# A gate's matmuls moved into the attention's tail, the first rows on earlier bytes, gate scaling on ScalarE, and the first cross norms inside the last product of the output projection

## The chip, the cores and the metric

The kernel runs on one core of a Trainium2 chip. The metric is device microseconds of one execution: before the change 2441.82 us, the median of three runs (2439.93 to 2442.28). The engines are TensorE (PE in the profile; its weight loads are PEld), VectorE (DVE), ScalarE (ACT), GpSimd (POOL) and the two queues that start transfers here, SyncE's (SPq) and ScalarE's (ACTq).

## The reference, cut to what matters

One layer of a hybrid encoder, 1024 tokens by 1024 channels, all in float32:

```python
h = rmsnorm(x, norm_mix);  proj = h @ w_in            # q k v | z | x B C | dt | gate_a | gate_b
attn = windowed_gqa_sink(q, k, v, sink)               # 16 heads, |t-s| <= 128, ALiBi, sink logit
ssd  = ssd_branch(z, xbc, dt, ...)                    # two scans, 2048 channels
merged = sigmoid(gate_a) * (attn @ w_attn_branch) + sigmoid(gate_b) * (ssd @ w_ssd_branch)
x = x + merged @ w_out                                # "wo"
h = rmsnorm(x, norm_cross)
x = x + cross_attention(h, rmsnorm(mem, norm_mem), w_xq, w_xkv, w_xo)
x = x + square(relu(rmsnorm(x, norm_ffn) @ w_up)) @ w_down
out = rmsnorm(x, norm_final)
```

The change lies between the end of `attn` and the first products of `cross_attention`.

## The kernel before, in words

Products keep float32 accuracy by splitting each operand into a high half (rounded to the matmul's format) and a low half (the rest), and by issuing three matmuls: high by high, high by low, low by high. A weight of 128 by 1024 is made ready by `wload` and `split_in` (L60 to L75): a transfer into a `raw` tile (2 buffers) on SPq, a copy to the high half on ACT (L66), a subtraction for the low half on POOL (L67); the two halves take two of the 6 `wop` buffers. Activations are split by an ACT copy and a DVE subtraction.

**Attention** (`attn_phase`, L584): four groups of heads. Each computes q and k, then for eight blocks of 128 queries the scores (L667, L668), the softmax (DVE L669, ACT L675, POOL L680), transposes (L690), a split (ACT L693, DVE L694) and the values (L699, L700), and writes the block to DRAM (L707). After each group comes one gate block (`gate_block`, `ATT_GATES`): 48 matmuls of h by a slice of `w_in`, a tanh and a store. Here the order on all engines is made by a planner that works through a priority heap in program order with estimated durations, so a gate's matmuls fill places where it expects PE to be idle. All tiles of this phase lie in one pool, `p2`, on the left side of the on-chip memory.

**Merge** (`merge_phase`, L719). On PE the order is now the written one; the other engines and the SP queue keep the planner's order. Four steps follow each other:

1. The gates 14 and 15 (`END_GATES`, 96 matmuls, L735 to L742), while the rows of the first product are loaded: `Pair.load(j)`, j = 0 to 7, one row of y and one of `w_ssd_branch` each, 16 rows of 512 KB. The rows with j < 4 lie in `k1` (10 buffers in the pool `m3`, which reuses the bytes of `p2`), the others in `k2` (right side) and `wop`.
2. Two `Pair`s for `ssd @ w_ssd_branch`. A `Pair` is a product of two 1024-deep halves done in seven half-size products (Strassen-Winograd form, `ORDER` = 1, 2, 6, 5, 7, 3, 4), of 48 matmuls each (L1399). The operands of the next product are sums of quarters (`op`, L1316, DVE) and splits (`split`, ACT L1350 and DVE L1351), dealt out as `units` between the four groups of matmuls. The first product takes only rows with j < 4; `early(j)` makes four sums from the rows j and 4 + j.
3. `attn @ w_attn_branch`: two halves h of eight steps m, of 24 matmuls each. Each step needs one weight `wa` (`wa_load`, two steps ahead), and multiplies its result by a gate: `gate(m, h)` (L771) fetches a tile `g` (4 buffers) on SPq, and POOL turns the stored tanh into the sigmoid (L774). In the half h = 0 each step also splits a piece of `attn` for the other half (`at_split`), fetches and applies two gates 8 + m to the accumulator, and issues `p.load(m)` for `w_out` and the load of a row of x. In the half h = 1 each step does one of the eight units of the first split of `wo` (`split1`), and sums of `early`.
4. `merged @ w_out` as a third `Pair`, added into x.

**Cross attention** (`cross_phase`, L845): the planner orders PE again. Four norms and transposes of the rows 0 to 3 of x (`norm_tile`, L131, with its helpers up to L152: a square with sum on ACT, L127; a scale on DVE, L118; a power on POOL, L120; a product on DVE, L139; eight transposes on PE, L148; the split on ACT, L151, and DVE, L152), the splits of the keys and values kx and vx (two `wload`s with halves in `p3`), then `xq_unit(0, i)` (24 matmuls each on all four transposed rows) in turn with the norms of the rows 4 to 7. The norms' results `xn` of the rows 0 to 3 share two buffers (`ld`).

Of the kernel before, what the change touches and what calls it, by code (L numbers as in the profile page):

```python
# [16 lines left out]
P = 128  # L17
S = 1024
# [11 lines left out]
ATT_GATES = ((10,), (11,), (12,), (13,))  # L30
END_GATES = (14, 15)
# [552 lines left out]
def attn_phase(kx, ins, dr):  # L584
    nc, tc = kx.nc, kx.tc
    V, A, G, PE = nc.vector, nc.scalar, nc.gpsimd, nc.tensor
    with tc.tile_pool(name="p2", bufs=1) as ap:
# [31 lines left out]
        for kv in range(4):  # L619
            if kv % 2 == 0:  # L620
                w = wload(kx, ins["wk"][kv // 2])
                ps = kx.pg.tile([P, S], F32, tag="g", name="kps")
                for h in range(2):
                    gemm_fm(kx, ps[:, h * 512:(h + 1) * 512], w, kx.hT[h])
                for s in range(2):
                    kh = ap.tile([P, S], F32R, tag="kh", bufs=2, name="kh")
                    kl = ap.tile([P, S], F32R, tag="kl", bufs=2, name="kl")
# [91 lines left out]
def merge_phase(kx, ins, dr, x1_open):  # L719
# [4 lines left out]
    with tc.tile_pool(name="m3", bufs=1, reuse_waits="tile") as fp, ExitStack() as right, \  # L724
            tc.manual_schedule(engines={mybir.EngineType.PE}):
        k2p = right.enter_context(tc.tile_pool(name="m3r", bufs=1, side="right", reuse_waits="tile"))
        acc = [fp.tile([P, S], F32, tag="acc", bufs=8, name="acc") for _ in range(8)]
        pools = {"k1": fp, "k2": k2p}
        pairs = [Pair(kx, fp, pools, ins["wsb"][8 * b:8 * b + 8], dr.y[8 * b:8 * b + 8]) for b in range(2)]
# [5 lines left out]
        gw = [wload(kx, ins["wg"][m]) for m in END_GATES]  # L735
        for j in range(8):
            p.load(j)
        gps = [[bank() for _ in range(2)] for _ in END_GATES]
        pin_next_matmul(kx)
        for h in range(2):  # L740
            for w, ps in zip(gw, gps):
                gemm_fm(kx, ps[h], w, kx.hT[h])  # L742
        for m, ps in zip(END_GATES, gps):
            gt = kx.tabp.tile([P, 2, 512], F32, tag="tab", bufs=1, name="gt")
            for h in range(2):
                A.activation(gt[:, h], ps[h], AF.Tanh, scale=0.5)
                nc.scalar.dma_start(dr.gt[m][h], gt[:, h])
# [22 lines left out]

        def gate(m, h):  # L771
            g = fp.tile([P, 512], F32, tag="g", bufs=4, name="g")
            nc.sync.dma_start(g, dr.gt[m][h])
            G.tensor_scalar(g, g, 1.0, 0.5, ALU.add, ALU.mult)  # L774
            return g
# [25 lines left out]
        right.close()  # L801
        atk[1] = act_tiles(kx)
        kx.x1 = []
        x1p = x1_open()
        p = Pair(kx, fp, pools, None, [ins["wo"][k] for k in range(8)], acc)
        split1, early = None, None
        for h in range(2):
            for m in range(8):
                if h == 0:
                    at_split(1, m)  # L810
                    for hh in range(2):
                        g = gate(8 + m, hh)
                        V.tensor_tensor(half(m, hh), half(m, hh), g, ALU.mult)
# [21 lines left out]
                if 8 * h + m + 2 < 16:  # L835
                    wa_load((m + 2) % 8)

# [4 lines left out]
        p.products(bank, lambda i: p.units(i, None), add)  # L842


def cross_phase(kx, ins, dr):  # L845
    nc, tc = kx.nc, kx.tc
    V, A, G, PE = nc.vector, nc.scalar, nc.gpsimd, nc.tensor
    with tc.tile_pool(name="p3", bufs=1, reuse_waits="tile") as mp:
# [6 lines left out]
        def norm(h, j, grow, dst):  # L855
            xn = t4f("xn") if grow is not g_cross else mp.tile([P, D], F32, tag="ld", bufs=2, name="xn")
            norm_tile(kx, mp, kx.x1[4 * h + j], xn, grow, dst[h], j * P)

        g_cross = load_row(kx, kx.tabp, ins["gcross"], "tab")
        h2T = [act_tiles(kx)]  # L860
        for j in range(4):
            norm(0, j, g_cross, h2T)
# [6 lines left out]
        kxh, kxl = split_kv(dr.kx, "kx")  # L869
        vxh, vxl = split_kv(dr.vx, "vx")  # L870
# [414 lines left out]
class Pair:  # L1285
# [5 lines left out]
    def __init__(self, kx, fp, pools, us, ws, u=None):  # L1291
        self.kx, self.fp, self.pools, self.us, self.ws = kx, fp, pools, us, ws
        self.u, self.w, self.xy = u or [None] * 8, [None] * 8, [None] * 4

    def row(self, tag, src):
        if tag == "wop":
            t = self.kx.wp.tile([P, D], F32, tag="wop", bufs=6, name="row")
        else:
            t = self.pools[tag].tile([P, D], F32, tag=tag, bufs={"k1": 10, "k2": 6}[tag], name="row")
# [3 lines left out]
    def load(self, j):  # L1303
        if self.us is not None:
            self.u[j] = self.row("k1" if j < 4 else "k2", self.us[j])
        self.w[j] = self.row("k1" if j < 4 or self.us is None else "wop", self.ws[j])
# [11 lines left out]
    def early(self, j):  # L1318
# [5 lines left out]
        else:  # L1324
            self.xy[j] = self.fp.tile([P, D], F32, tag="k1", bufs=10, name="xy")
# [79 lines left out]
def down_phase(kx, ins, dr, first, out):  # L1405
    nc, tc = kx.nc, kx.tc
    V, A, G, PE = nc.vector, nc.scalar, nc.gpsimd, nc.tensor
    with tc.tile_pool(name="p6", bufs=1, reuse_waits="tile") as fp, \
# [21 lines left out]
        pairs = [Pair(kx, fp, {"k1": fp, "k2": fp}, dr.u[m:m + 8], [ins["wdn"][k] for k in range(m, m + 8)])  # L1430
                 for m in (16, 24, 4)]
# [24 lines left out]
        for b, p in enumerate(pairs):  # L1456
            nxt = pairs[b + 1] if b < 2 else None
            if nxt is None:
                fraw, fw, fu = [None] * 8, [], []

                def fload(j):
                    fraw[j] = p.row("wop", ins["wdn"][12 + j])
                    fraw[4 + j] = p.row("k2", dr.u[12 + j])
# [38 lines left out]
def hybrid_encoder(ctx, tc, ins, out, dbg=None):  # L1502
# [33 lines left out]
    with tc.tile_pool(name="tabp", bufs=1) as kx.tabp:  # L1536
# [9 lines left out]
        merge_phase(kx, ins, dr, x1_open)  # L1546
        ok, grow = cross_phase(kx, ins, dr)
# [77 lines left out]
```

## Time and profile before

| | us |
|---|---|
| median of three runs | 2441.82 |
| the profiled execution | 2442.35 |
| its span, first to last instruction | 2440.6 |
| PE busy | 2339.8 (96%) |
| DVE, ACT, POOL busy | 1606.9, 1134.5, 928.9 |
| granted TensorE clock, mean | 0.988 |

A line of the timeline gives the start of an instruction (or of a run of like ones, xN), its duration, engine, source line, operation, output<-inputs, sizes, and in brackets the idle time of the engine just before it with what ended it. A line of the windows gives, for one stretch, the busy time and the number of instructions of each engine, the granted TensorE clock, the busy share of the DMA engines and their rate. Times are microseconds from the span's start.

### The profile page before, as it was taken

The page shows a single profiled execution, that of the slowest core. Times are in us where ns is not written, and L with a number is a line of the kernel's source. Part 1 is how long each engine was busy: PE and PEld are TensorE (multiplying, and loading weights), DVE is VectorE, ACT ScalarE, POOL GpSimd, SP SyncE. Part 2 cuts the span into 40 slices and gives each one's busy share as a digit, 9 for nine tenths or more (in the row PEclk, how much of TensorE's full clock was granted, in tenths as well). Part 3 has the DMA queues.
Part 4 walks back from the last instruction along what each step waited for, and adds up shares of the span by engine and source line. Part 5 has one row for each costly group of instructions (what it writes and reads, how often), then busy time and mean ns, then how long its engine had stood idle before and what let it go on. Part 6 is the DMA issues. An engine that isn't in the chain of part 4 may idle for free.

```text
span 2440.6 us, 32397 instructions
## 1 busy us (share of the span) xinstructions
PE 2339.8 (96%) x11868; PEld 1941.6 (80%) x11868; DVE 1606.9 (66%) x2520; ACT 1134.5 (46%) x2406; POOL 928.9 (38%) x873
## 2 busy tenths in 40 slices
PE   7899999999999998999989999999998999999998
PEld 6687887878788787877767887878986887788887
DVE  5747576575756655356657888874676446689984
ACT  5436354454635444477765442244553333233442
POOL 4235445363543525245441015324485444200010
PEclk9999999999999999999999999999999999999999
DMA  6214132231413223111116256212243335731301
GB/s 220 81 61 128 55 112 87 73 115 57 127 57 110 82 77 97 40 52 49 41 42 224 104 168 228 70 44 70 86 152 133 104 121 160 255 155 70 130 26 69
DMA packets 150319, 252.07 MB, mean 103 GB/s; under 512 B 11280, under 2 KB 86160, under 8 KB 150160
## 3 DMA queue, kind: packets, MB, share of 16 engines
q1 hardware_dynamic: 79264, 211.19, 25.5%
q10 hardware_dynamic: 70896, 38.81, 5.6%
q8 instruction: 94, 1.54, 0.3%
q14 instruction: 65, 0.53, 0.1%
HBM read 202.51 MB, written 47.45 MB: 102 GB/s over the span
## 4 chain that ended last, share of the span: by engine, by line
PE 60%; DVE 14%; POOL 9%; ACT 8%; issue 6%; DMA 3%; ACTq 0%; POOLq 0%; SPq 0%; DVEq 0%
PE dps L1399 9%; PE mps L1399 8%; PE pb L1191 6%; PE pc L1191 3%; PE zp L85 2%; PE zp L81 2%; PE zp L86 2%; PE st L462 2%; POOL wlo L67 2%; DVE cx L350 2%; POOL prev L477 2%; POOL cb_t L476 1%; ACT whi L66 1%; PE dps L85 1%; PE dps L81 1%
## 5 line engine op out<-in xcount | busy, mean ns | idle before, releaser
L67 POOL TENSOR_TENSOR wlo<-raw,whi 128x1024 fp32r<-128x1024 f32 x110 | 271.9, 2473 | 471.8 <-ACT whi L66 442.5
L1350 ACT ACTIVATE kt<-row 128x512 fp32r<-128x512 f32 x264 | 144.2, 620 | 187.3 <-PE dps L1399 82.9
L1399 PE MATMUL mps<-kt 128*128 128x512 f32 x1008 | 229.0, 389 | 0.0
L1399 PE MATMUL dps<-kt 128*128 128x512 f32 x1008 | 228.6, 389 | 0.0
L81 PE MATMUL cps<-kt,whi 128*128 128x512 f32 x512 | 217.1, 424 | 8.6 <-DVE cx L350 8.6
L1399 PEld LDWEIGHTS mps<-kt 128*128 128x128 f32 x1008 | 189.2, 188 | 39.5 <-DVE kt L1351 0.4
L1399 PEld LDWEIGHTS dps<-kt 128*128 128x128 f32 x1008 | 189.2, 188 | 39.3
L66 ACT ACTIVATE whi<-raw 128x1024 fp32r<-128x1024 f32 x112 | 118.0, 1055 | 199.2 <-DMA raw<-in_wa_dram 48.8
L86 PE MATMUL cps<-kt,wlo 128*128 128x512 f32 x512 | 200.8, 392 | 0.0
L85 PE MATMUL cps<-kt,whi 128*128 128x512 f32 x512 | 200.4, 391 | 0.0
L1351 DVE TENSOR_TENSOR kt<-row,kt 128x512 fp32r<-128x512 f32 x264 | 176.3, 715 | 7.1 <-ACT kt L1350 7.0
L81 PEld LDWEIGHTS cps<-kt,whi 128*128 128x128 f32 x512 | 97.1, 190 | 34.9 <-issue 16.3
L120 POOL TENSOR_TENSOR rr<-rv,mhalf 128x1 f32<-128x1 f32 (+1 forms) x50 | 38.5, 771 | 220.9 <-DVE rv L118 218.1
L1137 POOL TENSOR_TENSOR wop<-w,wop 128x512 fp32r<-128x512 f32 x64 | 86.1, 1346 | 85.9 <-ACT wop L1136 74.4
L85 PEld LDWEIGHTS cps<-kt,whi 128*128 128x128 f32 x512 | 97.1, 190 | 26.1 <-issue 7.3
L86 PEld LDWEIGHTS cps<-kt,wlo 128*128 128x128 f32 x512 | 96.8, 189 | 21.0
L496 ACT ACTIVATE ef<-rows,ebias 128x128 f32<-128x128 f32 x256 | 83.2, 390 | 53.3 <-PE cb L511 49.8
L1191 PE MATMUL pb<-kt,wop 128*128 128x512 f32 x384 | 96.3, 399 | 11.0 <-ACT c L1245 9.4
L669 DVE CUSTOM_DVE_ANT_0 t<-sps,bias 128x384 f32<-128x384 f32 (+1 forms) x128 | 64.3, 521 | 55.1 <-PE sps L668 53.7
L497 ACT ACTIVATE eb<-rows,ebias 128x128 f32<-128x128 f32 x256 | 84.3, 392 | 34.9 <-POOL rows L488 34.9
L680 POOL TENSOR_SCALAR t<-t,den 128x384 f32<-128x384 f32 (+1 forms) x128 | 69.1, 559 | 82.0 <-DVE den L678 65.5
L1077 POOL TENSOR_TENSOR wd<-row,wd 128x1024 fp32r<-128x1024 f32 x4 | 11.2, 2803 | 228.4 <-ACT wd L1076 228.4
(368 smaller groups left out, 6572.8 us busy)
## 6 DMA issues: line engine op xcount, KB each, us to landing
rows<-d_cs ACTq DMA_DIRECT2D x128, 256.0 KB, 3.8
raw<-in_wssd_dram SPq DMA_DIRECT2D x48, 512.0 KB, 3.8
raw<-in_wup_dram SPq DMA_DIRECT2D x40, 512.0 KB, 3.9
d_u<-c SPq DMA_DIRECT2D x64, 256.0 KB, 2.4
row<-in_wdn_dram SPq DMA_DIRECT2D x28, 512.0 KB, 6.2
row<-d_u SPq DMA_DIRECT2D x28, 512.0 KB, 6.7
x<-in_x_dram SPq DMA_DIRECT2D x16, 512.0 KB, 5.9
raw<-in_wg_dram SPq DMA_DIRECT2D x16, 512.0 KB, 3.7
```

What stands on the lines that cost most here:

```text
L66: nc.scalar.activation(hi, raw, AF.Copy)
L67: (eng or nc.gpsimd).tensor_tensor(lo, raw, hi.bitcast(F32), ALU.subtract)
L81: i = mm(out, l[0], r[0], start=first, stop=False)
L85: mm(out, l[0], r[1], start=False, stop=False)
L86: mm(out, l[1], r[0], start=False, stop=last)
L496: A.activation(ef[:, h], rows[:, 0, h], AF.Exp, bias=kx.ebias[:, b, j, 0, o:o + 1])
L497: A.activation(eb[:, h], rows[:, 1, h], AF.Exp, bias=kx.ebias[:, b, j, 1, o:o + 1])
L1137: self.kx.nc.gpsimd.tensor_tensor(t[:, 1], src, t[:, 0].bitcast(F32), ALU.subtract)
L1191: self.kx.nc.tensor.matmul(ps, w[:, i, ks], act[:, k, j], start=start and k == 0 and m == 0, stop=k == 3 and m == 2, skip_group_check=True)
L1350: nc.scalar.activation(t[:, j, 0], src, AF.Copy)
L1351: nc.vector.tensor_tensor(t[:, j, 1], src, t[:, j, 0].bitcast(F32), ALU.subtract)
L1399: self.kx.nc.tensor.matmul(ps[t], lt[:, k, x, ts], rt[:, k, y], start=n in (1, 2, 5) and k == 0 and m == 0, stop=k == 3 and m == 2, skip_g ...
```

## The change

- `ATT_GATES` gives gate 14 to the last group of attention; the merge begins with gate 15 alone.
- The tiles `kh`, `kl` and `q` of attention move from `p2` to a pool `p2r` on the right side. They are last read by the last scores. The merge's new pool of eight rows `kr` lies on the right side, where `p2r` was. The rows j < 4 of the first pair (the operands of the first product) go to `kr`, the rows of y with 4 + j to `k` (8 buffers, in `m3`), those of the weight to `wop`.
- `gate` scales on ACT (a copy with scale and bias) in place of POOL.
- `p.load(m)` and the load of x move from the half h = 0 to the half h = 1; `split1` and two of the four `early` sums of each j move from all eight steps of h = 1 to its last four. Two tiles of sums (`xy`, j = 2 and 3) of the third pair go to `wop` in place of `k1`.
- The four norms of the rows 0 to 3 start in the units of the last product of `wo`, with four `xn` buffers; the transposes of the rows 0 and 1 stand on PE before the third and fourth group of its matmuls, those of the rows 2 and 3 right after its last matmul.
- The splits of kx and vx move behind the four `xq_unit(0, i)` and the norms of the rows 4 to 7.
- `Pair` takes a function that gives rows; `down_phase` passes one that does as before.

```diff
-ATT_GATES = ((10,), (11,), (12,), (13,))
-END_GATES = (14, 15)
+ATT_GATES = ((10,), (11,), (12,), (13, 14))
+END_GATE = 15
...
-    with tc.tile_pool(name="p2", bufs=1) as ap:
+    with tc.tile_pool(name="p2", bufs=1) as ap, tc.tile_pool(name="p2r", bufs=1, side="right") as aq:
...
-                    kh = ap.tile([P, S], F32R, tag="kh", bufs=2, name="kh")
+                    kh = aq.tile([P, S], F32R, tag="kh", bufs=2, name="kh")
...
-                    q = ap.tile([P, S], F32R, tag="q", bufs=6, name="q")
+                    q = aq.tile([P, S], F32R, tag="q", bufs=6, name="q")
...
+        def row(tag):
+            pool, bufs = {"k": (fp, 8), "kr": (kr, 8), "wop": (kx.wp, 6)}[tag]
+            return pool.tile([P, D], F32, tag=tag, bufs=bufs, name="row")
+
+        tags = [(["kr"] * 4 + ["k"] * 4, ["kr"] * 4 + ["wop"] * 4),
+                (["k"] + ["kr"] * 3 + ["k"] * 4, ["k"] + ["kr"] * 3 + ["wop"] * 4)]
...
         def at_load(k):
-            t = fp.tile([P, S], F32, tag="k1", bufs=10, name="at")
+            t = row("k" if k in (0, 1, 6, 7) else "kr")
...
-            G.tensor_scalar(g, g, 1.0, 0.5, ALU.add, ALU.mult)
+            A.activation(g, g, AF.Copy, bias=0.5, scale=0.5)
...
+                if h == 0 and m == 7:
+                    right.close()
+                    x1p = x1_open()
+                if h == 1:
                     p.load(m)
                     xt = x1p[m // 4].tile([P, D], F32, tag="x1", bufs=4, name="x1")
                     nc.sync.dma_start(xt, ins["x"][m * P:(m + 1) * P])
                     kx.x1.append(xt)
-                else:
                     if m == 0:
                         split1 = p.split(1)
                         early = [p.early(j) for j in range(4)]
-                    split1[m]()
-                    if m < 4:
-                        early[m][1]()
-                        early[m][3]()
+                    if m >= 4:
+                        j = m - 4
+                        split1[2 * j]()
+                        split1[2 * j + 1]()
+                        early[j][1]()
+                        early[j][3]()
...
+        def units_of(i):
+            units = p.units(i, None)
+            if i == 6:
+                h2T.extend(act_tiles(kx))
+                xns = [row("k") for _ in range(4)]
+                for j in range(4):
+                    norm_rows(kx, fp, kx.x1[j], xns[j], g_cross)
+                units = [lambda: None] * 2
+                units += [lambda j=j: norm_split(kx, xns[j], h2T, j * P) for j in range(2)]
+                kx.late = lambda: [norm_split(kx, xns[j], h2T, j * P) for j in range(2, 4)]
+            return units
+
+        p.products(bank, units_of, add)
+        kx.late()
+    return h2T, g_cross
...
-        for j in range(4):
-            norm(0, j, g_cross, h2T)
...
-        kxh, kxl = split_kv(dr.kx, "kx")
-        vxh, vxl = split_kv(dr.vx, "vx")
...
         for i in range(4):
             xq_unit(0, i)
             norm(1, i, g_cross, h2T)
+        kxh, kxl = split_kv(dr.kx, "kx")
+        vxh, vxl = split_kv(dr.vx, "vx")
...
-            self.xy[j] = self.fp.tile([P, D], F32, tag="k1", bufs=10, name="xy")
+            self.xy[j] = self.row("wop")
```

More of the change, by code (lines that the diff above doesn't have):

```diff
@@ L725, in merge_phase @@
             tc.manual_schedule(engines={mybir.EngineType.PE}):
-        k2p = right.enter_context(tc.tile_pool(name="m3r", bufs=1, side="right", reuse_waits="tile"))
+        kr = right.enter_context(tc.tile_pool(name="m3r", bufs=1, side="right", reuse_waits="tile"))
         acc = [fp.tile([P, S], F32, tag="acc", bufs=8, name="acc") for _ in range(8)]
-        pools = {"k1": fp, "k2": k2p}
-        pairs = [Pair(kx, fp, pools, ins["wsb"][8 * b:8 * b + 8], dr.y[8 * b:8 * b + 8]) for b in range(2)]
+        def row(tag):
[3 more added lines that the diff above has]
+                (["k"] + ["kr"] * 3 + ["k"] * 4, ["k"] + ["kr"] * 3 + ["wop"] * 4)]
+        pairs = [Pair(kx, fp, row, ins["wsb"][8 * b:8 * b + 8], dr.y[8 * b:8 * b + 8], *tags[b]) for b in range(2)]
         p = pairs[0]
@@ L733, in bank @@
             return kx.pp.tile([P, 512], F32, tag="p", name="mps")
-        gw = [wload(kx, ins["wg"][m]) for m in END_GATES]
+        gw = wload(kx, ins["wg"][END_GATE])
         for j in range(8):
             p.load(j)
-        gps = [[bank() for _ in range(2)] for _ in END_GATES]
+        gps = [bank() for _ in range(2)]
         pin_next_matmul(kx)
         for h in range(2):
[L741 to L747, printed above, removed]
+            gemm_fm(kx, gps[h], gw, kx.hT[h])
+        gt = kx.tabp.tile([P, 2, 512], F32, tag="tab", bufs=1, name="gt")
+        for h in range(2):
+            A.activation(gt[:, h], gps[h], AF.Tanh, scale=0.5)
+            nc.scalar.dma_start(dr.gt[END_GATE][h], gt[:, h])
         for unit in p.split(1) + [u for j in range(4) for u in p.early(j)]:
@@ L769, in wa_load @@
             wa.append(wload(kx, ins["wa"][m]))
+        kx.x1 = []
         def gate(m, h):
@@ L800, in merge_phase @@
             p.products(bank, units_of, add)
-        right.close()
         atk[1] = act_tiles(kx)
-        kx.x1 = []
-        x1p = x1_open()
-        p = Pair(kx, fp, pools, None, [ins["wo"][k] for k in range(8)], acc)
+        p = Pair(kx, fp, row, None, ins["wo"], None, ["k"] * 8, acc)
         split1, early = None, None
@@ L836, in merge_phase @@
                     wa_load((m + 2) % 8)
+        g_cross = load_row(kx, kx.tabp, ins["gcross"], "tab")
         def add(n, t, ch, ps):
@@ L840, in add, with cross_phase @@
             V.tensor_tensor(xh, xh, ps, ALU.add)
-        p.products(bank, lambda i: p.units(i, None), add)
-def cross_phase(kx, ins, dr):
+        h2T = []
+        def units_of(i):
[12 more added lines that the diff above has]
+    return h2T, g_cross
+def cross_phase(kx, ins, dr, h2T, g_cross):
     nc, tc = kx.nc, kx.tc
@@ L855, in norm @@
         def norm(h, j, grow, dst):
-            xn = t4f("xn") if grow is not g_cross else mp.tile([P, D], F32, tag="ld", bufs=2, name="xn")
+            xn = t4f("xn")
             norm_tile(kx, mp, kx.x1[4 * h + j], xn, grow, dst[h], j * P)
-        g_cross = load_row(kx, kx.tabp, ins["gcross"], "tab")
-        h2T = [act_tiles(kx)]
-        for j in range(4):
-            norm(0, j, g_cross, h2T)
+        h2T = [h2T]
         def split_kv(src, nm):
@@ L1289, with __init__, fetch @@
     ORDER = (1, 2, 6, 5, 7, 3, 4)
-    def __init__(self, kx, fp, pools, us, ws, u=None):
-        self.kx, self.fp, self.pools, self.us, self.ws = kx, fp, pools, us, ws
+    def __init__(self, kx, fp, row, us, ws, ut, wt, u=None):
+        self.kx, self.fp, self.row, self.us, self.ws, self.ut, self.wt = kx, fp, row, us, ws, ut, wt
         self.u, self.w, self.xy = u or [None] * 8, [None] * 8, [None] * 4
[L1295 to L1299, printed above, removed]
+    def fetch(self, tag, src):
+        t = self.row(tag)
         self.kx.nc.sync.dma_start(t, src)
@@ L1304, in load @@
         if self.us is not None:
-            self.u[j] = self.row("k1" if j < 4 else "k2", self.us[j])
-        self.w[j] = self.row("k1" if j < 4 or self.us is None else "wop", self.ws[j])
+            self.u[j] = self.fetch(self.ut[j], self.us[j])
+        self.w[j] = self.fetch(self.wt[j], self.ws[j])
     def half(self, name, j):
@@ L1428, in deal, with row @@
                 unit()
-        pairs = [Pair(kx, fp, {"k1": fp, "k2": fp}, dr.u[m:m + 8], [ins["wdn"][k] for k in range(m, m + 8)])
-                 for m in (16, 24, 4)]
+        def row(tag):
+            pool, bufs = {"k1": (fp, 10), "k2": (fp, 6), "wop": (kx.wp, 6)}[tag]
+            return pool.tile([P, D], F32, tag=tag, bufs=bufs, name="row")
+        pairs = [Pair(kx, fp, row, dr.u[m:m + 8], ins["wdn"][m:m + 8], ["k1"] * 4 + ["k2"] * 4,
+                      ["k1"] * 4 + ["wop"] * 4) for m in (16, 24, 4)]
         p = pairs[0]
@@ L1461, in fload @@
                 def fload(j):
-                    fraw[j] = p.row("wop", ins["wdn"][12 + j])
-                    fraw[4 + j] = p.row("k2", dr.u[12 + j])
+                    fraw[j] = p.fetch("wop", ins["wdn"][12 + j])
+                    fraw[4 + j] = p.fetch("k2", dr.u[12 + j])
                 def fsplit_w(j):
@@ L1545, in hybrid_encoder @@
         kx.pp = ctx.enter_context(tc.tile_pool(name="p8", bufs=8, space=PSUM, reuse_waits="tile"))
-        merge_phase(kx, ins, dr, x1_open)
-        ok, grow = cross_phase(kx, ins, dr)
+        h2T = merge_phase(kx, ins, dr, x1_open)
+        ok, grow = cross_phase(kx, ins, dr, *h2T)
         with tc.manual_schedule(engines={mybir.EngineType.PE}):
```

2 lines of the change are left out of this document (1 added, 1 removed).

## The prediction

> **What bounds the kernel now.** I read first the page's engine sums: PE is busy 96% of the span, so about 101 us without matmuls are all that can be had without removing matmuls. Next I cut the stretch that the change touches into stages.
>
> ```profile
> span 2440.6 us, 32397 instructions
> PE 2339.8 (96%) x11868; PEld 1941.6 (80%) x11868; DVE 1606.9 (66%) x2520; ACT 1134.5 (46%) x2406; POOL 928.9 (38%) x873
> ...
> core 0: us, PE busy (x) PEld busy (x) DVE busy (x) ACT busy (x) POOL busy (x), PEclk, DMA share, GB/s
> 1240.00:1262.00 22.00, 21.56 (x111) 16.67 (x110) 16.91 (x62) 17.45 (x55) 11.22 (x18) 1.00 0.03 7
> 1262.00:1292.20 30.20, 21.01 (x108) 14.32 (x109) 17.01 (x51) 22.60 (x57) 14.98 (x21) 1.00 0.24 75
> 1292.20:1314.00 21.80, 21.80 (x98) 18.02 (x97) 13.32 (x22) 7.86 (x13) 1.29 (x1) 1.00 0.84 313
> 1314.00:1467.00 153.00, 153.00 (x676) 126.46 (x675) 133.30 (x209) 72.15 (x133) 16.43 (x11) 1.00 0.45 158
> 1467.00:1563.20 96.20, 90.58 (x384) 73.49 (x383) 81.74 (x83) 24.17 (x33) 53.74 (x37) 0.96 0.53 179
> 1563.20:1639.20 76.00, 76.00 (x337) 62.87 (x337) 58.18 (x88) 29.94 (x52) 10.13 (x6) 1.00 0.07 22
> 1639.20:1660.40 21.20, 15.11 (x63) 12.11 (x62) 11.93 (x18) 9.91 (x18) 5.21 (x6) 0.68 0.16 50
> 1660.40:1720.00 59.60, 59.48 (x334) 51.28 (x333) 32.87 (x62) 34.95 (x91) 31.38 (x35) 1.00 0.24 80
> ```
>
> The rows are: attention with gate 13 as filler; its tail without filler; the gates 14 and 15; the two pairs; the sixteen steps of `wa`; `wo`; the first cross norms with the first `xq_unit`; the rest of `xq`. PE has no gap in the pairs and in `wo`. The pairs give the price of a matmul, 153.0/672 = 0.2277 us (two times seven products of 48), and there DVE is busy 133.3 of 153, so it keeps up. Three stages lose time: the tail 30.20 - 21.01 = 9.2 us; `wa`, 96.2 against 384 x 0.2277 = 87.4, 8.8 us; and the stretch of the norms. Each is an end of a chain through other engines, and what PE gains in one stage the gap-free stage behind it passes on.
>
> **The tail: one gate moves in, the rows come earlier.** Gate 14 is 48 matmuls, 10.9 us; they leave the stage behind the tail (21.8 becomes 10.9) and fill its gaps. Filled perfectly, 9.2 us are gained. The stretch before shows what filling does: with gate 13's matmuls in it PE idled 0.44 us of 22.0. Its two tanh, two stores and one weight load move too; each is there already, and no weight was split in the tail before, the last whi being at 1233.9.
>
> ```profile
> 1276.38 0.49 PE L699 MATMUL op<-ph,vhl 128*128 128x512 f32 x1 [3.31 <-ACT ph L693]
> ...
> 1279.20 0.28 PE L668 MATMUL sps<-kl,q 128*128 128x256 f32 x1
> ...
> 1291.86 0.50 PE L700 MATMUL op<-pl,vhl 128*128 128x512 f32 x1 [0.23 <-DVE pl L694]
> ```
>
> The largest gap, 3.31 us, waits for ACT; ACT is busy 22.6 of 30.2 there, and the tanh add 2 x 0.6. The filler also puts up to 0.4 us before links of that chain. I take 2.2 us of the gaps as left: **7.0 us gained**, bounds 0 (the chain is stretched by as much as is filled) to 9.2.
>
> This holds only if the first product's rows are there in time, because the cover shrinks by 10.9 us.
>
> ```profile
> 1267.53 27.96 SPq L707 DMA_DIRECT2D d_at<-oa  x6
> 1295.60 0.63 SPq L1300 DMA_DIRECT2D row<-in_wsb_dram  x1
> ```
> ```profile
> 1299.82 0.69 DVE L1316 TENSOR_TENSOR xy<-row 128x512 f32<-128x512 f32 x1 [8.02 <-DMA row<-in_wsb_dram]
> 1310.71 1.29 DVE L1351 TENSOR_TENSOR kt<-row,kt 128x512 fp32r<-128x512 f32 x2
> ```
>
> Now they start at 1295.6, behind `p2`'s last use and behind the last of attention's stores on the queue, and DVE ends the first split at 1312.0, 2 us before the product. In the new place they wait for the last scores, 1279.5 (the second row of the tail's fence), 16 us earlier. Eight rows of 524 KB at 313/0.84 = 373 GB/s take 11.3 us, so they are in at about 1291 to 1293, and the split needs eight ACT copies and eight DVE subtractions of 0.6 us, mostly meanwhile. Gate 15 ends at 1314.0 - 7.0 = 1307: 14 us of room. The other eight rows then need 11.3 us from 1293 on and are used by the second product at 1318; DVE has 28 sums and splits at 0.6 to 0.7 us, 18 us, by then. Close, but earlier than now, where the gates' weights hold `wop` to 1314.
>
> **The `wa` steps.** 24 matmuls are 5.46 us; a step now takes 96.2/16 = 6.01.
>
> ```profile
> L86 PE MATMUL mps<-kt,wlo 128*128 128x512 f32 x128 | 51.5, 402 | 5.6 <-POOL wlo L67 5.6
> ...
> L67 POOL TENSOR_TENSOR wlo<-raw,whi 128x1024 fp32r<-128x1024 f32 x13 | 33.7, 2591 | 2.4 <-ACT whi L66 2.4
> ...
> L774 POOL TENSOR_SCALAR g<-g 128x512 f32<-128x512 f32 x24 | 20.7, 865 | 36.8 <-DMA g<-d_gt 30.5 <-DVE xy L1316 4.1 <-DVE row L1316 2.1
> ...
> L66 ACT ACTIVATE whi<-raw 128x1024 fp32r<-128x1024 f32 x13 | 13.8, 1061 | 61.0 <-DMA raw<-in_wa_dram 44.4 <-PE mps L85 12.3 <-POOL wlo L67 3.3
> ...
> L1350 ACT ACTIVATE kt<-acc 128x512 fp32r<-128x512 f32 x8 | 4.4, 618 | 10.6 <-PE mps L86 10.6
> ```
> ```profile
> 1522.01 0.80 PE L86 MATMUL mps<-kt,wlo 128*128 128x512 f32 x1 [3.68 <-POOL wlo L67]
> 1522.61 0.63 PE L81 MATMUL mps<-kt,whi 128*128 128x512 f32 x1
> ```
>
> PE waits 5.6 us for the low halves; after the 3.68 us gap the clock is down (0.96 for the stage), which is the rest of 8.8. POOL stands 30.5 us waiting for gate tiles, with the low halves queued behind; this goes. Its 32 scalings become ACT copies of 0.62 us (the L1350 row: the same size, from on-chip memory), 19.8 us on an engine busy 24.2 of 96.2. The row and x loads, 1 MB a step, go from h = 0 to h = 1: h = 0 falls from three `g`, `wa`, a row and x (2.4 MB) to 1.3 MB a step. What is added: a copy that waits for its `g` holds the whi queued behind it on ACT; and two `wop` buffers hold sums, so h = 1 has two weight pairs in place of three. A pair's refill is 1.06 + 2.59 = 3.7 us in a step of 5.46, so it fits.
>
> ```profile
> 1477.07 0.68 DVE L813 TENSOR_TENSOR acc<-acc,g 128x512 f32<-128x512 f32 x1
> 1487.90 2.88 DVE L813 TENSOR_TENSOR acc<-acc,g 128x512 f32<-128x512 f32 x1
> ```
> ```profile
> 1487.25 0.62 POOL L774 TENSOR_SCALAR g<-g 128x512 f32<-128x512 f32 x1 [2.09 <-DVE row L1316]
> 1487.83 2.40 POOL L67 TENSOR_TENSOR wlo<-raw,whi 128x1024 fp32r<-128x1024 f32 x1
> ```
> ```profile
> g<-d_gt SPq DMA_DIRECT2D x32, 256.0 KB, 3.5
> ```
>
> The same DVE product takes 0.68 alone and 2.88 when POOL's low half starts just before. The scaling released both at once, every step. The four `g` buffers are the second loop: landing 3.5, scaling 0.62, product 0.68 to 2.88, so 4.8 to 7.0 us for two of a step's three tiles, and one whole step more (5.5) for the third. Three tiles over four buffers: (2 x 4.8 + 10.3)/4 = 5.0 us a step, or (2 x 7.0 + 12.5)/4 = 6.6 if every product meets a low half. Only the first is under 5.46. Each step has five DVE products and one low half, so I take one in three: **6.0 us gained**, bounds 0 and 8.8.
>
> The first split of `wo` and the sums are now pressed into the last four steps: two splits, three sums and two gate products, seven DVE operations of 0.68, 4.8 us of a step's 5.46. In the two of these steps with a low half 2.2 come on top, so DVE falls 1.5 us behind in each and regains 0.7 in each of the last two. What hides the rest is that the first group of `wo`'s product reads its slices in order, 0.7 us apart; uncovered, up to 1.6 us are lost, inside the bounds above.
>
> The page "SBUF — State Buffer" of the Trainium skill (section "Who interferes with whom") says that a DVE instruction with two on-chip inputs and a GpSimd instruction that reads there lock each other out for a whole instruction. The 0.68 and 2.88 agree, and by this rule the collisions stay, as the low halves stay on POOL.
>
> **The end of `wo` and the norms.**
>
> ```profile
> 1639.19 1.91 PE L148 MATMUL nt<-ident,xn 128*128 128x128 f32 x16
> 1645.94 3.98 PE L148 MATMUL nt<-ident,xn 128*128 128x128 f32 x16 [4.84 <-DVE rv L118]
> ...
> 1660.40 0.38 PE L148 MATMUL nt<-ident,xn 128*128 128x128 f32 x2
> ```
> ```profile
> 1628.50 49.47 SPq L65 DMA_DIRECT2D raw<-in_wxq_dram  x8
> ```
> ```profile
> 1626.40 3.17 DVE L139 SCALAR_TENSOR_TENSOR xn<-x,rr,grow 128x1024 f32<-128x1024 f32 x1
> 1644.60 1.29 DVE L139 SCALAR_TENSOR_TENSOR xn<-x,rr,grow 128x1024 f32<-128x1024 f32 x1 [0.66 <-POOL rr L120]
> ```
> ```profile
> 1622.03 1.07 ACT L127 ACTIVATE xn<-x 128x1024 f32<-128x1024 f32 x1
> 1640.67 2.04 ACT L151 ACTIVATE kt<-nt 128x512 fp32r<-128x512 f32 x4
> ```
>
> Two norms are done early; the other two wait for the two `ld` buffers until PE has transposed, and PE waits 4.84 us and then runs at half speed: sixteen transposes 3.98 against 1.91. The stretch from 1639.2 to 1660.4 does 38 transposes (1.91/16 each, 4.5 us) and 24 matmuls (5.5): 10.0 us of work in 21.2. With four buffers the norms start at 1622, as the first does now, and need each 1.1 on ACT, 0.6 on POOL and 1.3 on DVE (3.2 beside a low half): at most 4 x 5 = 20 us, by 1642 in today's times, while the last transposes come at 1639.2 + 1.9 = 1641. The first `xq_unit` then waits only for the last split, 0.6 + 0.7 and hand-overs, 1.5 us: 10.0 + 1.5 = 11.5. **9.5 us gained**, bounds 5 (the gap of 4.84 comes back) and 11.2 (no wait at all). Moving kx and vx frees the `raw` buffers for the weights of `xq`, which start at 1628.5 now, and costs nothing: POOL is busy 31.4 of 59.6 in the `xq` stage, which hides the two low halves (4.8 us) before the first scores need them; uncovered they are 4.8.
>
> A gap of 3.31 us in the tail left the clock up, 3.68 and 4.84 brought it down. "TensorE: Matmul & The Clock Gate" of the Trainium skill (section "What's actually happening") has a window of about 3.4 us for it; the trace agrees.
>
> **Sum.** Against the profiled execution (2442.35, with 1.75 around its span; it lies 0.5 above the median): 2442.35 - 7.0 - 6.0 - 9.5 = 2419.85, forecast **2420**.
>
> **Rivals.**
>
> *The rows are not earlier* (15%): the queue orders them behind the attention's stores, the last of which went just before 1295.6, so DVE ends its split at 1312.0 as today and the front gains at most 2.0: 2442.35 - 2.0 - 15.5 = 2425. For it: the order of the queue now. Against: until then the rows had no free bytes, so nothing was to be gained by another order.
>
> *`wa` gains nothing* (15%): the low halves go on locking DVE, two pairs leave less slack, ACT takes the waits for `g` that POOL had: 2442.35 - 16.5 = 2426.
>
> *ScalarE becomes the bound of the `wa` steps, slower* (7%): the copy waits a landing of 3.5 us with the next whi behind it, then 0.62 + 1.06 + 2.59, plus two splits 1.24: a refill of 9.0, over two pairs (9.0 + 5.5)/2 = 7.25 us a step, 16 x 1.24 = 19.8 more than now, against 16.5 gained elsewhere: 2446. It decides from 6.01 + 16.5/16 = 7.04 us a step. Against: h = 1 needs one `g` a step with four buffers, so it is fetched long before.
>
> *The norms don't fit* (8%): an `xn` is late inside the last product, where PE's order is written, a gap there over 3.5 us drops the clock again and the stretch gains 3: 2426.
>
> The forecast itself has 55%. The measurement tells about 0.2%, 4.9 us. Three of the rivals are still faster; with all three at once 2442.35 - 2.0 - 0 - 3.0 = 2437, the edge of telling. **Faster 0.85, same 0.08, slower 0.07.** The range joins the upper bounds of the gains (9.2 + 8.8 + 11.2, 2413) and two rivals together (2442.35 - 2.0 - 9.5 = 2431 and the like), widened by 2 below and 5 above for an order of the planner that no row shows: 2411 to 2436.
>
> **What would show it.** Gate matmuls between the values of the tail and less than 3 us idle there; the first row issued near 1280; the first product near 1307; `wa` in 88 to 92 us without a gap over 3.4; ACT's scalings at 0.6 us; sixteen transposes inside the last product and the first `xq_unit` done 11 to 13 us after it. The forecast is wrong if the tail lengthens, if whi waits behind scalings on ACT, or if the gained time comes back as a wait further on, in the `up` stage, where PE is held by weights.

## The result, and the profile after

The changed kernel takes 2460.15 us (median of four runs, 2456.06 to 2463.13) against 2442.05 of the kernel before beside it (2439.93 to 2442.45): ratio 1.0075, with a 95% interval of 1.0057 to 1.0092. It is slower; the forecast of 2420 and the whole range, up to 2436, were wrong.

The windows of the kernel after, cut at the same places of the program: attention with its filler, the tail, gate 15, the two pairs, the sixteen `wa` steps, `wo` with the first norms, and the `xq` units.

```profile
span 2457.1 us, 32385 instructions
...
PE 2346.7 (96%) x11868; PEld 1946.2 (79%) x11868; DVE 1602.4 (65%) x2520; ACT 1153.6 (47%) x2438; POOL 903.7 (37%) x841
```
```profile
1240.00:1262.00 22.00, 21.53 (x112) 16.88 (x111) 16.48 (x61) 16.82 (x52) 11.04 (x18) 1.00 0.03 7
1262.00:1293.20 31.20, 30.20 (x157) 22.68 (x155) 19.53 (x54) 23.49 (x60) 15.14 (x22) 1.00 0.53 168
1293.20:1304.50 11.30, 11.30 (x51) 9.26 (x50) 6.00 (x11) 7.17 (x13) 1.37 (x2) 1.00 0.93 326
1304.50:1458.50 154.00, 152.93 (x674) 126.01 (x673) 137.61 (x219) 76.76 (x140) 7.64 (x3) 1.00 0.42 145
1458.50:1558.90 100.40, 91.55 (x386) 73.77 (x386) 73.21 (x80) 38.93 (x59) 37.88 (x14) 0.95 0.56 194
1558.90:1636.80 77.90, 77.90 (x354) 64.62 (x353) 62.95 (x99) 32.20 (x58) 7.30 (x6) 1.00 0.05 18
1636.80:1725.10 88.30, 66.41 (x291) 54.71 (x290) 32.28 (x48) 31.71 (x69) 30.76 (x27) 0.85 0.19 59
```

PE is still busy 96% and has the same 11868 matmuls; the stages tell where the time went. The front does what was foretold: the tail's idle time falls from 9.2 to 1.0 us and the first product starts at 1304.6, 9.4 us earlier. Then it is lost three times: 1.4 us in the pairs (1.1 of them a wait for a split at the second product), 3.7 us in the `wa` steps, which were to become shorter, and 19.9 us in the `xq` stage. `wo` is 1.8 longer, which is its sixteen transposes (1.91). In all 9.4 - 1.4 - 3.7 - 1.8 - 19.9 = -17.4: 17.4 us are lost at the last `xq` matmul, 16.5 at the end of the span.

PE's timeline of the kernel after, the rows with the long waits:

```profile
1532.48 0.80 PE L81 MATMUL mps<-kt,whi 128*128 128x512 f32 x1 [5.32 <-ACT whi L66]
...
1650.81 1.94 PE L148 MATMUL nt<-ident,xn 128*128 128x128 f32 x8 [5.32 <-DVE xn L139]
...
1663.79 1.94 PE L148 MATMUL nt<-ident,xn 128*128 128x128 f32 x8 [3.95 <-DVE xn L139]
...
1677.12 1.94 PE L148 MATMUL nt<-ident,xn 128*128 128x128 f32 x8 [3.95 <-DVE xn L139]
...
1688.98 1.07 PE L148 MATMUL nt<-ident,xn 128*128 128x128 f32 x8 [3.95 <-DVE xn L139]
```

In the `xq` stage PE waits four times, 17.2 us, for the norms of the rows 4 to 7, and the clock goes down with it (0.85 for the stage). ACT's timeline says why: first the kernel before, then the kernel after.

```profile
1648.44 1.05 ACT L127 ACTIVATE xn<-x 128x1024 f32<-128x1024 f32 x1
...
1650.44 1.05 ACT L127 ACTIVATE xn<-x 128x1024 f32<-128x1024 f32 x1
...
1661.38 0.58 ACT L878 ACTIVATE xq<-xqp 128x512 fp32r<-128x512 f32 x1
```
```profile
1646.31 0.58 ACT L898 ACTIVATE xq<-xqp 128x512 fp32r<-128x512 f32 x1
1646.79 1.05 ACT L127 ACTIVATE xn<-x 128x1024 f32<-128x1024 f32 x1
...
1659.88 0.60 ACT L898 ACTIVATE xq<-xqp 128x512 fp32r<-128x512 f32 x1 [6.43 <-PE xqp L86]
1660.37 1.05 ACT L127 ACTIVATE xn<-x 128x1024 f32<-128x1024 f32 x1
```

Before, the squares of the rows 4 and 5 (L127) run ahead of the first unit's copy. After, each square stands right behind the copy of a unit, so a norm begins only when the unit ahead of its transposes has ended, and PE waits out the whole norm: square, power, product. The change has one line on this that its list does not name and that the prediction passed over: in `norm`, the tile `xn` of the rows 4 to 7 no longer comes from the two buffers `ld` but from `yk`, the tag of the units' own results. (A tag names a set of buffers that tiles of one kind share in turn.)

In the `wa` steps the first eight run without a gap; all is lost within 1506 to 1537. There the queue of SP with the chief wait on it (from 1495 to 1545: the total, how often, the longest), ACT, one row of DVE and two of POOL read:

```profile
1516.76 6.45 SPq L779 DMA_DIRECT2D g<-d_gt  x2
1523.32 0.37 SPq L65 DMA_DIRECT2D raw<-in_wa_dram  x1
```
```profile
SPq L779 <- DVE acc L840: 18.1, 6, 5.6
```
```profile
1525.64 0.63 ACT L780 ACTIVATE g<-g 128x512 f32<-128x512 f32 x1 [4.20 <-DVE row L1335]
1530.85 0.63 ACT L780 ACTIVATE g<-g 128x512 f32<-128x512 f32 x1 [4.58 <-DMA g<-d_gt]
1531.38 1.04 ACT L66 ACTIVATE whi<-raw 128x1024 fp32r<-128x1024 f32 x1
```
```profile
1514.03 6.89 DVE L1370 TENSOR_TENSOR kt<-row,kt 128x512 fp32r<-128x512 f32 x4
```
```profile
1513.50 2.86 POOL L67 TENSOR_TENSOR wlo<-raw,whi 128x1024 fp32r<-128x1024 f32 x1 [3.88 <-ACT whi L66]
1516.52 2.65 POOL L67 TENSOR_TENSOR wlo<-raw,whi 128x1024 fp32r<-128x1024 f32 x1 [0.16 <-ACT whi L66]
```

DVE works through the splits and sums of `wo` (four splits in 6.89 us, beside two low halves on POOL), and the products with `g` (L839, L840) stand behind them. So the four `g` tiles stay taken: the queue waits for L840 before it can issue a transfer into `g` (18.1 us in this stretch), two of these transfers take it 6.45 us, and the weight's transfer stands behind them. Then the scaling on ACT waits 4.58 us for its `g` with the weight's high half behind it, and PE waits 5.32 us for that half.

### The profile page after: what moved, and what is told of

Same layout as the page of the kernel before. It is cut to its first block, busy times and chain, and to the rows that moved or that the text cites. A ratio compares the mean times of both kernels' runs of the same rounds, so it can differ in the third digit from the quotient of the medians.

```text
span 2457.1 us, 32385 instructions
## 1 busy us (share of the span) xinstructions
PE 2346.7 (96%) x11868; PEld 1946.2 (79%) x11868; DVE 1602.4 (65%) x2520; ACT 1153.6 (47%) x2438; POOL 903.7 (37%) x841
## 4 chain that ended last, share of the span: by engine, by line
PE 58%; DVE 14%; POOL 9%; ACT 8%; issue 7%; DMA 4%; ACTq 0%; SPq 0%; POOLq 0%; DVEq 0%
PE dps L1418 9%; PE mps L1418 8%; PE pb L1213 6%; PE pc L1213 3%; PE zp L85 2%; PE zp L81 2%; PE zp L86 2%; PE st L462 2%; POOL wlo L67 2%; POOL prev L477 2%; DVE cx L350 1%; ACT whi L66 1%; POOL cb_t L476 1%; DMA g<-d_gt 1%; PE dps L81 1%
## 5 line engine op out<-in xcount | busy, mean ns | idle before, releaser
L86 PEld LDWEIGHTS cps<-kt,wlo 128*128 128x128 f32 x512 | 97.3, 190 | 21.2
L81 PE MATMUL gps<-kt,whi 128*128 128x512 f32 x240 | 103.0, 429 | 0.0
```

Of the source, the lines that this page charges most:

```text
L81: i = mm(out, l[0], r[0], start=first, stop=False)
L86: mm(out, l[1], r[0], start=False, stop=last)
```

## The experiments

Every run starts from the kernel after. The stages are read from PE's timeline of each run: `wa` from its first matmul to its last, `wo` and `xq` from the last matmul of the stage before to their own last; the median is that of the timed runs. The first product starts between 1301.7 and 1305.0 in these runs, although no edit lies ahead of it. Why was not looked into, so the stages tell more than a small difference of two medians.

| run | first product at | `wa` | `wo` | `xq` | median us |
|---|---|---|---|---|---|
| before | 1314.0 | 96.7 | 76.2 | 68.4 | 2442.05 |
| after | 1304.6 | 100.4 | 77.9 | 88.2 | 2460.15 |
| `xn` in `ld` (c1) | 1302.6 | 101.3 | 77.9 | 70.3 | 2439.15 |
| kx, vx first (c2) | 1301.7 | 100.2 | 78.0 | 96.9 | 2467.84 |
| both (c3) | 1303.5 | 99.5 | 77.9 | 69.0 | 2439.33 |
| scaling on POOL (w1) | 1302.7 | 100.1 | 77.9 | 88.2 | 2458.86 |
| c1, kx and vx in a tag of their own (d5) | 1302.2 | 101.0 | 78.0 | 56.3 | 2427.05 |
| d5, eight `g` (d5_g8) | 1304.4 | 87.2 | 79.0 | 56.4 | 2416.68 |
| d5, DVE in written order (e2) | 1304.9 | 93.1 | 81.3 | 56.4 | 2424.23 |
| e2, eight `g` (e3) | 1305.0 | 91.4 | 82.9 | 56.4 | 2425.78 |
| d5_g8, scaling on POOL (f1) | 1302.8 | 92.1 | 78.8 | 56.4 | 2421.02 |
| after, eight `g` (f3) | 1304.8 | 87.2 | 79.7 | 85.5 | 2447.42 |

### Whose fault is the `xq` stage

**`xn` back in `ld`.**

```diff
-            xn = t4f("xn")
+            xn = t4f("xn") if grow is not g_cross else mp.tile([P, D], F32, tag="ld", bufs=2, name="xn")
```

> The kernel after, with one line changed: the norms of rows 4 to 7 take their result tile from the two buffers `ld`, as in the kernel before, and not from the 16 buffers of `yk`, from which the results of the xq units are taken too. Three theories of the 19.9 us that the xq stage (from the end of wo to the last matmul of xq: 67.7 us before, 87.6 after) lost. Slot order: the tiles of one tag are handed out in the written order, so the square of row 4 + i stands behind the copy of unit i on ACT; with the tag of its own the squares of rows 4 and 5 run ahead of the first copy, the four waits of 5.32, 3.95, 3.95 and 3.95 us and the half clock behind them go, and the stage takes 57 to 62 us: 2429 to 2435 in all. Late weights: what costs is that kx and vx hold the two raw buffers, so at most the half of the loss comes back and the norms still wait: 2450 to 2458. Early units: the units now start before any norm of rows 4 to 7 can be done, whatever their tiles: the same four waits, 2456 to 2461.

Measured 2439.15 (ratio to before 0.9987, 0.9978 to 0.9996), 21 us under the kernel after. All four waits for norms are gone, so early units and late weights fall as the chief cause. But the stage is 70.3, not 57 to 62: other waits came in the place of the old ones. PE, ACT, the queue and a wait of the queue (from 1640 to 1670) of this run:

```profile
1666.11 0.50 PE L81 MATMUL xsp<-kxh,xq 128*128 128x256 f32 x2 [1.73 <-ACT kxh L66]
1668.53 0.39 PE L85 MATMUL xsp<-kxl,xq 128*128 128x256 f32 x1 [1.92 <-POOL kxl L67]
...
1674.21 0.80 PE L81 MATMUL xqp<-kt,whi 128*128 128x512 f32 x1 [3.83 <-ACT whi L66]
...
1677.73 0.79 PE L86 MATMUL xqp<-kt,wlo 128*128 128x512 f32 x1 [2.30 <-POOL wlo L67]
```
```profile
1663.54 0.60 ACT L898 ACTIVATE xq<-xqp 128x512 fp32r<-128x512 f32 x1 [4.75 <-PE xqp L86]
...
1664.98 1.07 ACT L66 ACTIVATE kxh<-raw 128x1024 fp32r<-128x1024 f32 x1
```
```profile
1599.98 0.33 SPq L65 DMA_DIRECT2D raw<-d_kx  x1
1647.94 0.33 SPq L65 DMA_DIRECT2D raw<-d_vx  x1
```
```profile
SPq L65 <- POOL kxl L67: 20.2, 1, 20.2
```

kx is loaded from 1600 on, yet its high half, whose tile is a `yk` too, is written behind the copies of all four units. From 1648 until then kx and vx hold both `raw` tiles, and no weight can be loaded: the queue waits 20.2 us for the low half of kx.

**kx and vx ahead of the units, without and with `ld`.**

```diff
+        kxh, kxl = split_kv(dr.kx, "kx")
+        vxh, vxl = split_kv(dr.vx, "vx")
         for i in range(4):
             xq_unit(0, i)
             norm(1, i, g_cross, h2T)
-        kxh, kxl = split_kv(dr.kx, "kx")
-        vxh, vxl = split_kv(dr.vx, "vx")
```

> The kernel after, with the splits of kx and vx written ahead of the xq units again, as before; the norms' tiles stay in `yk`. Slot order: the four waits for norms stay; only the two waits for weights at the end of the stage (0.92 and 2.82 us) go, 2455 to 2458. Late weights: the stage falls from 87.6 to 70 or less, 2440 or less. Early units: as slot order.

> Both: the norms' tiles in `ld` and the splits of kx and vx ahead of the units, so that cross attention differs from the kernel before only by the first four norms. Slot order: the waits for norms go and those for weights too, unless kx and vx now delay the first unit's weights: 2427 to 2433, up to 4 us under the run with `ld` alone. Late weights: as the run with kx and vx alone. Early units: 2452 to 2458.

c2 is 2467.84, 7.7 us slower than the kernel after; none of the three theories had that. The four waits for norms stay, as slot order said (now 5.3 us each), but in place of the small waits for weights comes a larger one at the start (8.90 us for a high half, 1.21 for a low one). c3 has it alone and lands at 2439.33, above the 2427 to 2433 expected; PE's timeline of c3:

```profile
1646.33 0.79 PE L81 MATMUL xqp<-kt,whi 128*128 128x512 f32 x1 [9.39 <-ACT whi L66]
...
1649.27 0.80 PE L86 MATMUL xqp<-kt,wlo 128*128 128x512 f32 x1 [1.72 <-POOL wlo L67]
```

Ahead of the units, kx and vx hold the two `raw` tiles until their halves are written, at 1637.59 and later, when `wo` has ended (1635.2), and the first weight is late. That the halves wait for bytes which `wo` still uses is the likely reason; it was not tested. So with the old tags neither place is free: the first one costs 9.39 + 1.72 us (two waits at the first unit), the last one 9.8 (the four rows of c1).

**A tag of their own for kx and vx.**

```diff
-            return mp.tile([P, 2, 512], F32R, tag="yk", bufs=16, name=name)
+            return mp.tile([P, 2, 512], F32R, tag="yk", bufs=12, name=name)
...
-            hi = t4k(nm + "h").rearrange("p a b -> p (a b)")
-            lo = t4k(nm + "l").rearrange("p a b -> p (a b)")
+            hi, lo = [mp.tile([P, 1024], F32R, tag="kv", bufs=4, name=nm + x) for x in "hl"]
```

> The kernel after with the norms' tiles in `ld`, and the four halves of kx and vx in a tag of their own (`kv`, 4 buffers; `yk` has 12 in place of 16; the bytes are the same), written where the kernel after has them. In the run with `ld` alone the high half of kx stood on ACT behind the copies of all four units (1664.98, though its raw tile was loaded from 1600 on), both raw tiles were held by kx and vx to 1668, and PE waited 1.73, 1.92, 3.83 and 2.30 us for kx and for weights. Slot order: it was the tag again; now the high half of kx runs ahead of the first copy, the raw tiles go round, and the xq stage falls from 70.25 to 57 to 62 us: 2426 to 2431 in all. Rival, too many splits for two raw tiles: ten weights in 60 us hold PE wherever they stand, and the stage stays at 66 or more: 2435 to 2440.

2427.05, ratio 0.9933 (0.9918 to 0.9948): the stage takes 56.3 us without a wait of 0.8 us or more. ACT's timeline of this run has kx ahead of the first copy:

```profile
1639.69 1.08 ACT L66 ACTIVATE kxh<-raw 128x1024 fp32r<-128x1024 f32 x1
...
1644.59 0.58 ACT L897 ACTIVATE xq<-xqp 128x512 fp32r<-128x512 f32 x1
```

The ten splits are the same in the same stage, so their number was not the limit. What c1 and d5 show is that the tag, with the number of buffers that goes with it, moves an instruction ahead of the copies or behind them; nothing else is changed in them. That the planner hands out the tiles of one tag in written order is the reading that fits the five orders seen; the planner itself was not looked into.

### Whose fault are the `wa` steps

**The scaling back on POOL.**

```diff
-            A.activation(g, g, AF.Copy, bias=0.5, scale=0.5)
+            G.tensor_scalar(g, g, 1.0, 0.5, ALU.add, ALU.mult)
```

> The kernel after, with the scaling of the gates back on POOL and nothing else. It asks what made the sixteen wa steps 3.6 us longer (96.65 to 100.2) instead of 6 us shorter. In the trace after PE has no gap in the first eight steps and loses all in a stretch of 30 us in the second eight, where DVE is busy without a pause. If the copies on ScalarE are the cause (each waits for its g with the weight's high half queued behind), the steps fall below 96: 2451 to 2456. If DVE is (the sums and splits of wo pressed together, so that the g tiles come free late and the transfers behind them on the queue start late), POOL's scalings take over the wait and the first eight steps lose what they lost before: 101 to 109 us, 2461 to 2469.

2458.86; the steps take 100.1 in place of 100.4. Neither number came: in this kernel it makes no difference which engine scales, since whichever does it waits for the late `g`, and a half of the weight waits behind it (PE's longest wait is 5.38 for POOL's low half where it was 5.32 for ACT's high half).

**Eight `g` tiles, on d5.**

```diff
-            g = fp.tile([P, 512], F32, tag="g", bufs=4, name="g")
+            g = fp.tile([P, 512], F32, tag="g", bufs=8, name="g")
```

> The same with eight g buffers in place of four. It asks why the wa steps take 100 us in the kernel after: in the stretch that loses, the transfers of g wait on the queue 6.45 and 2.85 us for a free buffer with the weight's transfer behind them, then the scaling waits for its g with the weight's high half behind it. Queue theory: with free buffers the weight is not held, and the steps fall from 100 to 90 to 95 us, 5 to 10 us less than the run without this edit. Rival, DVE itself: its 22 us without a pause hold PE by another way (banks, the low halves), and the time is within 2 us of that run.

2416.68, ratio to before 0.9888 (0.9871 to 0.9904), 10.4 us under d5, a little more than the 5 to 10 that the queue theory gave. The window of its `wa` steps, and a row of DVE:

```profile
1458.40:1545.60 87.20, 87.20 (x386) 72.21 (x385) 67.29 (x73) 34.75 (x52) 38.91 (x14) 1.00 0.61 205
```
```profile
1508.70 6.91 DVE L1369 TENSOR_TENSOR kt<-row,kt 128x512 fp32r<-128x512 f32 x4
```

PE has no gap in the sixteen steps. DVE is packed as before, with the same four splits in 6.91 us: late products are harmless as long as they hold no transfer. The gap went with the buffers, not with DVE's load.

**DVE in the written order, with the split spread.** The loop is put under the manual order for DVE as well as PE.

```diff
-        for h in range(2):
-            for m in range(8):
+        with tc.manual_schedule(engines={mybir.EngineType.PE, mybir.EngineType.DVE}):
+            for h in range(2):
+                for m in range(8):
...
+                        split1[m]()
                         if m >= 4:
                             j = m - 4
-                            split1[2 * j]()
-                            split1[2 * j + 1]()
```

> As the run with `kv`, four g buffers, but in the sixteen wa steps the order on DVE is the written one too, not the planner's, and the split of wo is written one unit a step over all eight steps of the second half, so that no step has more than six operations of DVE. DVE theory (the planner packs eight splits and twelve sums of wo ahead of the gates' products in four steps): no g comes free late, and the steps take 88 to 93 us: 7 to 12 us less than the run with `kv` alone. Rival, two weight pairs in place of three: the refill of 3.7 us in a step of 5.5 is what is late, and no more than 2 us are gained.

> The written order on DVE, the spread split and eight g buffers together. If the late g tiles were the one cause, the two mends are two ways to the same end, and this is within 2 us of the better of them. If the second pair or the locking of DVE and POOL is a cause of its own, each mend gives a part and both together more than either.

The first missed: 2424.23, only 2.8 under d5. PE's timeline of e2:

```profile
1525.94 0.50 PE L81 MATMUL mps<-kt,whi 128*128 128x512 f32 x1 [1.67 <-ACT whi L66]
...
1557.26 7.10 PE L1417 MATMUL mps<-kt 128*128 128x512 f32 x30 [3.04 <-DVE kt L1369]
```

The steps do fall, from 101.0 to 93.1, so DVE's order and the spread of the split, which this run changes together, were a part of it; but with four `g` tiles the weight still waits, and 3.3 us come back at the start of `wo`, since the planner's early split had hidden that wait. With eight `g` tiles too (2425.78) nothing is gained on e2, and it is 9 us over d5_g8, which neither expectation had: the two mends aren't two ways to the same end, and the planner's order is the better one once the buffers are there.

**Scaling on POOL with eight `g` tiles.** The edit of w1 on d5_g8.

> The run with `kv` and eight g buffers, with the scaling of the gates on POOL again. It asks what the move to ScalarE itself is worth once no g is late. The prediction's step: POOL's scalings (0.62 to 0.87 us, three a step in the first half) hold the low halves queued behind them and lock DVE: the wa steps go from 87.2 to 91 or more, 2420 to 2426. Rival: with eight buffers every g lands long before, POOL (one low half of 2.6 us and at most three scalings in 5.46 us) has room, and the time stays within 2 us of 2416.7.

2421.02, as the prediction's step had it: 4.3 us slower than d5_g8, steps of 92.1. The move to ScalarE has a worth, but only now. POOL and PE of this run:

```profile
1497.22 0.62 POOL L780 TENSOR_SCALAR g<-g 128x512 f32<-128x512 f32 x1 [4.70 <-DMA g<-d_gt]
1497.81 5.16 POOL L67 TENSOR_TENSOR wlo<-raw,whi 128x1024 fp32r<-128x1024 f32 x2
```
```profile
1500.21 0.50 PE L86 MATMUL mps<-kt,wlo 128*128 128x512 f32 x1 [1.90 <-POOL wlo L67]
```

**Eight `g` tiles on the kernel after itself.**

> The kernel after with eight g buffers and nothing else. If the loss in the wa steps and the one in the xq stage have nothing to do with each other, this takes away the first alone, 13 us by the trace of the run with both mends (100.2 to 87.2): 2445 to 2450. If the time given back in the wa steps is lost again in the xq stage (weights that come later for it), 2452 or more.

2447.42, ratio 1.0020 (1.0011 to 1.0029), inside the 2445 to 2450 expected: steps of 87.2, `xq` still 85.5. The two losses are independent to 2.7 us in the `xq` stage, and neither mend alone accounts for all of it.

## Why the prediction was wrong

The step that failed most is a cost put at nothing: the norms of the rows 4 to 7, in the `xq` stage that lost 19.9 us. The second is the wait for `g` in the second half of the `wa` steps, which lost 3.7 us where 6.0 were to be gained. The tail came out as forecast, and somewhat better.

**The tail** gained 9.4 us where 7.0 was forecast and 9.2 was the upper bound. 1.0 us of idle time was left where 2.2 was assumed. The tail itself became 1.0 us longer (31.2 against 30.2), which the prediction had named as a sign of being wrong, but it holds 48 matmuls more. The tail and the gates behind it were also busy 1.3 us less with the same matmuls (21.01 + 21.80 before, 30.20 + 11.30 after), which the sum did not have. The rows, though, came later than its working had them. SP's waits from 1262 to 1305, and a row of ACT:

```profile
SPq L707 <- POOL oa L705: 30.8, 7, 5.7
```
```profile
1298.57 0.64 ACT L1369 ACTIVATE kt<-row 128x512 fp32r<-128x512 f32 x1 [0.27 <-DMA row<-in_wsb_dram]
```

The first row of `w_ssd_branch` was issued at 1275.69, 4 us ahead of the last scores (1279.78). But the queue waited 30.8 us for what attention's stores (L707) take from POOL, and rows stood behind these stores, as the first rival said: a row that the first split needs was issued at 1293.88, and its copy on ACT came at 1298.57. So the "14 us of room" were not there. The split's last subtraction ended at 1305.9, behind the product's first matmul at 1304.6, and PE did not wait, as it reads the slices in order. DVE worked without a pause from 1298.57 on, and the second product waited 0.84 us for its split, the place that the prediction called "Close". The pairs gave back 1.4 us.

**The `wa` steps**: 6.0 us of gain foretold, 3.7 lost. The step that failed is the sentence against the third rival: "h = 1 needs one `g` a step with four buffers, so it is fetched long before". The prediction put the press of the four buffers into the first half, where the steps then ran without a gap; it counted DVE's lag in the second half (1.5 us) but not what that lag holds: the `g` tiles, the queue, the next weight. It also read "the last four steps" from the written order, while the planner drew all eight splits of `wo` forward to 1510 to 1521. Rival three had the right picture, a high half queued behind a scaling that waits, but as a rate for all sixteen steps (7.25 us a step); the long wait happened once, for 5.32 us, with the half clock behind it and three waits of 1.0 to 1.3 us for low halves. The bound itself was right: with eight `g` tiles the steps take 87.2, and 9.5 us are gained (9.0 against the window of 96.2 from which the bound of 8.8 was taken), of which the engine of the scaling is 4.3 by median. The 6.0 is not what the working gives: with one product in three beside a low half the round of the buffers takes 5.5 us a step, which is some 8 us gained; 6.0 is near two thirds of the bound.

**The norms in `wo`** went as said: sixteen transposes inside the last product and sixteen behind it without a wait, the first unit at 1639.0, 2.1 us after its end. In d5_g8 the stage with its transposes gains 68.4 - 56.4 - 1.9 = 10.1 us, where 9.5 was forecast (its own rows, 21.2 - 11.5, give 9.7). What failed is that the working ended at the first unit. The norms of the rows 4 to 7 were not costed at all: their lead of one unit lay in two squares that ran before the first copy, and a changed tag took it away. That is 17.9 us of the stage by the run with `ld`, 21.0 by the median.

**"Moving kx and vx ... costs nothing: POOL is busy 31.4 of 59.6"** failed too. POOL had room (30.76 busy of 88.30 in the kernel after); the scarce thing was the pair of `raw` tiles, held until the halves have their place. That is 14.0 us of the stage by d5 against c1, 12.1 by the median.

Had the cross attention's tags and the `g` buffers been as in d5_g8, the sum would have been right to 3 us (2419.85 against 2416.68), but in part by luck: in d5_g8 the three gains are 9.6, 9.5 and 10.1, in all 29.2 where 22.5 was forecast, and 3.9 of them are lost in stages that the sum held to be unchanged (1.5 of it in the pairs). The prediction forecast each stage for what it frees and took it for granted that the planner's order behind it stays. The closing sentence looked for returned time in the `up` stage; it was lost in the `wa` and `xq` stages, ahead of that.

The page "SBUF — State Buffer" of the Trainium skill, section "Who interferes with whom", says that a DVE instruction with two on-chip inputs and a GpSimd one that reads there lock each other out. The kernel after agrees: four splits, two of them beside POOL's low halves, took 6.89 us, and four of the same size with POOL at rest took 2.49, as DVE's timeline shows:

```profile
1299.18 2.49 DVE L1370 TENSOR_TENSOR kt<-row,kt 128x512 fp32r<-128x512 f32 x4
```

But in d5_g8 that cost is still there (6.91 us), and the gaps are gone.

## What to carry to other kernels

Where a planner orders the work, a tile's tag is part of the order: two kinds of tile in one tag can tie an early instruction to a late one, and a tag of its own can be had in the same bytes. Of a tile that a transfer fills, ask who frees it and what stands behind that transfer on its queue: a late consumer is harmless until it holds a buffer that the queue waits for. When a stage is made to start earlier, follow what it needs next until the lead that was there before is found again.

## What the runs showed of the hardware that was not expected

After gaps of the same length the clock did not fall at the same point. Behind the gap of 3.95 us that ended at 1677.12 eight transposes took 1.94 us, at half speed from the first; behind the one that ended at 1688.98 they took 1.07. The clock in the windows after that second gap:

```profile
1689.00:1690.20 1.20, 1.17 (x9) 0.97 (x9) 0.00 (x0) 0.55 (x2) 1.20 (x1) 1.00 0.19 34
1690.20:1692.00 1.80, 0.90 (x4) 0.90 (x5) 0.00 (x0) 0.54 (x2) 1.80 (x2) 0.51 0.74 264
```

It fell only when PE had already been at work for over a microsecond, and the next matmuls paid. Nor does the length of a gap say whether the clock falls. A gap of 3.04 us in e2 (to 1557.26) left it up, one of 3.05 in e3 (to 1555.84) brought it down. The first row is of e2, the others are of e3:

```profile
1552.53:1555.93 3.40, 1.69 (x8) 1.07 (x6) 3.33 (x4) 2.42 (x5) 2.38 (x1) 1.00 0.06 22
```
```profile
1552.72:1556.11 3.39, 0.34 (x2) 0.27 (x2) 3.35 (x4) 0.81 (x2) 1.19 (x1) 1.00 0.35 99
1556.13:1559.53 3.40, 3.40 (x9) 2.63 (x9) 3.40 (x7) 0.00 (x0) 0.00 (x0) 0.50 0.15 58
```

In each trace the changes of the clock lie on steps of 3.41 us. In the `xq` stage of the kernel after they come at 1649.29, 1656.12, 1662.94, 1669.77, 1676.60, 1680.01, 1690.25 and 1700.49, as narrow windows show. The gap of e3 lies almost whole in one step, with 0.34 us of work in it; that of e2 is shared by two, with 1.69 and 2.08. So the edge near 3.5 us that the prediction took from its gaps of 3.31 and 3.68 is not a rule. How much work in a step keeps the clock up stays open: a step with 1.61 us kept it (kernel after, from 1683.42), and one with 1.83 lost it (f3, from 1316.99, with two waits of no more than 0.83 us).

"TensorE: Matmul & The Clock Gate" of the Trainium skill, section "What's actually happening", says that the window which the gate looks at runs freely and is not tied to the work; the fixed steps, and falls at varying distance behind a gap, agree with that.
